# A short decoder trunk on one core: the weight buffers and the transposed branch outputs at another place modulo 1024 bytes

## The chip, the cores and the metric

The kernel runs on one core of a Trainium2 chip. The metric is device time in microseconds (us) of one execution. Three runs of the kernel before took 1026.52, 1027.38 and 1032.1 us, so the median is 1027.38.

## The reference, cut to what matters

Two layers act on 256 tokens of width 1024, all in float32. Each layer has a mixer and a feed-forward part:

```python
proj = einsum('bsd,dn->bsn', x, w_in)          # 11 parts: mLSTM q/k/v/o, DeltaNet qkv/z, two gates, ...
ha = mlstm(...);  hb = gated_delta(...)        # the two branches
y = sigmoid(gate_a) * (ha @ w_branch_a) + sigmoid(gate_b) * (hb @ w_branch_b)
x = layernorm(ALPHA * x + y @ w_out)
gt, up = split(x @ w_ffn_up)                   # 1024 -> 2 x 2816
x = layernorm(ALPHA * x + (silu(gt) * up) @ w_ffn_down)
```

Nearly all of the arithmetic is in the dense products with weights.

## The kernel before, in words

**Products.** A float32 product is made of three matmuls of the type float32r (`three`, L259): each operand is split into a rounded part (H) and the rest (L), and H.H, L.H and H.L are added up in PSUM. A matmul has a stationary operand, which a weight load of 128 columns brings into TensorE first, and a moving operand, which streams past it. The profile shows the two as PEld and PE.

**Weights.** They come from HBM in units of 128 x 1024 floats (`loading`, L213): a DMA into `raw`, a ScalarE copy that makes `wH`, a VectorE subtraction that makes `wL`. There is a ring of six pairs in the pool `hl` (L220). Further units go to spots that are free at the time: `wT0` to `wT3` in the pool `fix`, `wh0` to `wh2` in the pool of the feed-forward stage.

**Short and long matmuls.** In `chunkB` (L332) a 128-column slice of weights is stationary and the transposed activations (`xtH`, `xtL`, or the branch outputs `haH`/`haL` and `hbH`/`hbL`, transposed) move, 256 columns: the short matmuls. For each slice the order is H.H, L.H, H.L, so the weight loads are wH, wH, wL, and the streams xtH, xtL, xtH. In `chunkA` (L274) and `splitA` (L290) a 128-column slice of activations is stationary and 512 columns of weights move: the long matmuls. The second half of the last down projection is cut into pieces of 256 columns. The up projections (from 365 to 455 us and from 866 to 960 us) are chunkB in 9 of 11 chunks, 96 short matmuls each. The gate matmuls (`gates`, L415) are short ones whose stationary operand has 24 columns only.

**Order.** TensorE's order is written out by hand (`ORDER`, `PLAN`, L34 and L120). `arrange` (L1162) sets the order on VectorE, ScalarE and GpSimd from a cost per instruction (its element counts) and from which tiles share memory; where in memory a tile lies has no part in a cost.

**Places in SBUF.** Tiles of a pool lie one behind the other, each rounded up to 32 bytes a partition, in the order in which the program first asks for them; pools follow one another. `xtH` (8192 bytes a partition), `xtL` (8192), the constants (4096) and `x` (8192) are whole multiples of 1024, so all begin at the same place modulo 1024; call it 0. `mh` and `ph` (L172, L173) take 32 bytes each, so what follows begins at 64: the spots `T0` to `T3`, `raw`, the ring, all of whole multiples of 1024 bytes, and the pools M (mixer) and F (feed-forward), which begin at one address. In F come `lnp2`, `hH`, `hL` (multiples of 1024) and the spots `wh0` to `wh2`, all at 64. In M come `dm`, `TT`, `YY` (multiples of 1024), then `gnc` (4 bytes, so 32), `cw` (384), and the tags `vs` and `A`, at 64 + 32 + 384 = 480: `haH` and `hbH` lie there. Behind `A`, which is 32 bytes over a multiple of 1024, and `sv` (128 bytes), the other tags lie at 480 + 32 + 128 = 640, `C` among them: `haL` and `hbL`; the gate weights `wgH` and `wgL` too. The gate weights' slices are 96 bytes long, so they begin at 640, 736, 832, 928, then 0, 96, 192, 288. The transposed result of the branches' sum, `yH` and `yL`, has the spots `T0` and `T1`. A weight slice of 128 columns is 512 bytes, so it begins at its buffer's place or 512 after; a row of activations is 1024 bytes.

Of the kernel before, what the change touches and what calls it, by code (L numbers as in the profile page):

```python
# [12 lines left out]
F32 = mybir.dt.float32  # L13
# [4 lines left out]
P = 128  # L18
# [19 lines left out]
def chunk_order():  # L38
    return ORDER + ["wb", "wo"] + [f"up{j}" for j in range(UP)] + ["dn0", "dn1"]
# [93 lines left out]
class Net:  # L133
    def __init__(self, ctx, tc, a, dbg=None):
        self.tc, self.nc, self.a, self.dbg = tc, tc.nc, a, dbg
        nc = tc.nc
        self.fix = ctx.enter_context(tc.tile_pool(name="fix", bufs=1))
        self.raw = ctx.enter_context(tc.tile_pool(name="raw", bufs=4))
        self.hl = ctx.enter_context(tc.tile_pool(name="hl", bufs=6))
        self.pj = ctx.enter_context(tc.tile_pool(name="pj", bufs=4, space=bass.MemoryType.PSUM))  # L140
        self.sm = ctx.enter_context(tc.tile_pool(name="sm", bufs=4, space=bass.MemoryType.PSUM))
        self.dr = ctx.enter_context(tc.tile_pool(name="dr", bufs=2, space=bass.MemoryType.DRAM))
        self.u = 0
        self.clock = 0
        self.due = []
        self.lnt = {}
        self.ahead = []
        self.ring = 0
        self.busy = set()
        self.F = None  # L150
        self.t3 = False
        self.spots = {}
        n = 0
        for l in range(NL):
            for name in chunk_order():
                for i in range(COUNT.get(name, 4)):
                    spot = SPOTS.get((name, i))
                    if spot and (name != "va0" or l):
                        self.spots[n] = spot
                    n += 1  # L160
        fix = self.fix
        self.xt = [fix.tile([P, KT, S], F32R, name="xtH"), fix.tile([P, KT, S], F32R, name="xtL")]
        self.cst = fix.tile([P, 4 * P + 2 * S], F32, name="cst")
        c = self.cst
        self.idn = c[:, 0:P]
        self.tri = c[:, P:2 * P]
        self.one = c[:, 2 * P:3 * P]
        self.gm = c[:, 3 * P:4 * P]
        self.pm = c[:, 4 * P:4 * P + S]
        self.ei = c[:, 4 * P + S:4 * P + 2 * S]  # L170
        self.x = fix.tile([P, 2, D], F32, name="x")
        self.mh = fix.tile([P, 8], F32, name="mh")  # L172
        self.ph = fix.tile([P, 8], F32, name="ph")  # L173
        nc.gpsimd.memset(self.mh, -0.5)
        nc.gpsimd.memset(self.ph, 0.5)
        nc.vector.memset(self.x[:, 0, 0:P], 0.0)
        ps = self.sm.tile([P, 512], F32, name="sm")
        for i in range(WARM):
            self.mm(ps[:, 0:P], self.x[:, 0, 0:P], self.x[:, 0, 0:P], True, True)
# [235 lines left out]
    def gates(self, l, xt):  # L415
        nc, M = self.nc, self.M
        wg = M.tile([P, KT * 24], F32, name="wg", tag="jk", bufs=1)
        nc.sync.dma_start(out=wg, in_=self.a["wg"][l])
        sv = M.tile([P, 32], F32, name="sv")
        nc.sync.dma_start(out=sv, in_=self.a["sv"][l])  # L420
        wH = M.tile([P, KT * 24], F32R, name="wgH", tag="tmp")
        wL = M.tile([P, KT * 24], F32R, name="wgL", tag="dg")
# [475 lines left out]
    def mixer(self, l):  # L898
        nc, M, a = self.nc, self.M, self.a
        xt = self.xt  # L900
        mt = M.tile
# [9 lines left out]
            nc.gpsimd.memset(t, 0.0)  # L911
        st = [{}, {}]
        sm = {}
        self.gnc = mt([P, 1], F32, name="gnc")
        gates = self.gates(l, xt)
        cw = mt([P, 24, 4], F32, name="cw")
        self.gn = gn = mt([P, D], F32, name="gn", tag="vs", bufs=2)
# [12 lines left out]
        if l == 0:  # L930
            self.load_x()
            for n in range(2):
                pss = yield from self.chunkA(xt)
                for t in range(2):
                    put_v(n, t, pss[t])
                if n == 0:
                    self.load_c()
                    next(gates)
            consts()
        else:  # L940
            next(gates)
            consts()
            self.splitA(xt, [(4, 0), (4, 0)], put_v)
            self.t3 = False
# [413 lines left out]
```

## Time and profile before

| What | Value |
|---|---|
| Median of three runs | 1027.38 us (1026.52 to 1032.1) |
| The profiled execution: its own time | 1030.46 us |
| Its span, first to last instruction | 1028.5 us |
| TensorE matmuls, weight loads (busy) | 1011.6 us, 942.9 us |
| VectorE, ScalarE (busy) | 735.9 us, 596.8 us |
| Granted TensorE clock, mean | 0.999 |
| DMA | 183.61 MB, mean 179 GB/s |

Busy time of TensorE is the union of matmul records, whose ends are modelled: records of neighbouring matmuls overlap. How fast matmuls follow one another is read from their starts (the timeline) or from how many fall into a window, and the length of a record tells two paces apart.

### The profile page before, as it was taken

What the parts mean: (1) busy time and instruction counts of PE and PEld (TensorE: products, weight loads), DVE (VectorE), ACT (ScalarE), POOL (GpSimd) and SP (SyncE); (2) the same over time, 40 slices, a digit from 0 to 9 for tenths busy, and PEclk for the clock granted to TensorE, in tenths of its full rate; (3) what the DMA queues carried; (4) which work ended last, traced back from release to release, by engine and by line L of the source; (5) the groups of instructions that cost most, each with busy time, mean ns of one, the idle gap of its engine ahead of it and who ended that gap; (6) DMA issues with size and microseconds to landing.
All of it is one profiled execution on the core that took longest, in us unless ns stands there. A gap on an engine that the chain in (4) does not pass through costs nothing.

```text
span 1028.5 us, 18935 instructions
## 1 busy us (share of the span) xinstructions
PE 1011.6 (98%) x7474; PEld 942.9 (92%) x7474; DVE 735.9 (72%) x1313; ACT 596.8 (58%) x1110; POOL 46.9 (5%) x68
## 2 busy tenths in 40 slices
PE   8999999999999999999999999999999999999997
PEld 6999989989998899998889998998999989999886
DVE  4778998799668655556657699878985885555453
ACT  5658567866665445445545765767676554444440
POOL 1001000100000000000010100001000010000001
PEclk9999999999999999999999999999999999999999
DMA  8876235544556656667644742555355755666651
GB/s 272 286 218 197 71 134 185 185 143 138 175 184 241 204 166 189 199 187 229 217 128 154 261 148 82 188 170 159 101 191 159 257 189 179 190 187 187 185 164 41
DMA packets 57689, 183.61 MB, mean 179 GB/s; under 512 B 6657, under 2 KB 14337, under 8 KB 56961
## 3 DMA queue, kind: packets, MB, share of 16 engines
q1 hardware_dynamic: 50976, 179.13, 54.3%
q10 hardware_dynamic: 6624, 3.28, 1.2%
q8 instruction: 58, 0.95, 0.4%
q14 instruction: 31, 0.25, 0.1%
HBM read 181.21 MB, written 1.18 MB: 177 GB/s over the span
## 4 chain that ended last, share of the span: by engine, by line
PE 86%; DVE 7%; ACT 3%; DMA 2%; issue 1%; SPq 0%; POOL 0%; POOLq 0%; ACTq 0%; DVEq 0%
PE pj L257 78%; PE sm L257 6%; DMA raw<-in_ws 2%; DVE wL L233 1%; DVE stt L736 1%; DVE tmp L734 1%; PE sm L367 1%; ACT wH L232 1%; DVE cv L632 1%; PE sm L647 1%; DVE wt L551 0%; DVE ha L580 0%; POOL sq L576 0%; DVE vT L637 0%; PE sm L1092 0%
## 5 line engine op out<-in xcount | busy, mean ns | idle before, releaser
L233 DVE TENSOR_TENSOR wL<-raw,wH 128x1024 fp32r<-128x1024 f32 (+1 forms) x302 | 364.3, 1214 | 190.1 <-ACT wH L232 186.1
L232 ACT CAST wH<-raw 128x1024 fp32r<-128x1024 f32 (+1 forms) x302 | 314.7, 1044 | 228.0 <-PE pj L257 171.9
L257 PE MATMUL pj<-xtH,wH 128*128 128x256 f32 x1328 | 373.6, 281 | 0.0
L257 PE MATMUL pj<-xtH,wL 128*128 128x256 f32 x1328 | 368.9, 278 | 0.2 <-DVE wL L233 0.2
L257 PE MATMUL pj<-xtL,wH 128*128 128x256 f32 x1328 | 368.8, 278 | 0.0
L257 PEld LDWEIGHTS pj<-xtL,wH 128*128 128x128 f32 x1328 | 250.9, 189 | 0.3
L257 PEld LDWEIGHTS pj<-xtH,wH 128*128 128x128 f32 x1328 | 249.5, 188 | 0.9
L257 PEld LDWEIGHTS pj<-xtH,wL 128*128 128x128 f32 x1328 | 249.4, 188 | 0.4 <-DVE wL L233 0.4
L257 PE MATMUL pj<-wH,xtH 128*128 128x512 f32 x216 | 74.0, 403 | 3.0 <-ACT wH L232 2.9
L257 PE MATMUL pj<-wL,xtH 128*128 128x512 f32 x216 | 71.7, 392 | 0.1
L257 PE MATMUL pj<-wH,xtL 128*128 128x512 f32 x216 | 71.8, 392 | 0.0
L257 PE MATMUL pj<-wH,hH 128*128 128x512 f32 (+1 forms) x168 | 62.2, 370 | 0.0
L257 PE MATMUL pj<-wL,hH 128*128 128x512 f32 (+1 forms) x168 | 62.0, 369 | 0.0
L257 PE MATMUL pj<-wH,hL 128*128 128x512 f32 (+1 forms) x168 | 62.0, 369 | 0.0
L632 DVE SCALAR_TENSOR_TENSOR cv<-cu,cw,cv 128x255 f32<-128x255 f32 (+2 forms) x144 | 59.8, 475 | 2.9 <-ACT cv L630 2.8
L257 PEld LDWEIGHTS pj<-wH,xtH 128*128 128x128 f32 x216 | 39.4, 189 | 11.9 <-ACT wH L232 4.7
L257 PEld LDWEIGHTS pj<-wH,xtL 128*128 128x128 f32 x216 | 40.6, 188 | 9.1
L257 PEld LDWEIGHTS pj<-wL,xtH 128*128 128x128 f32 x216 | 40.5, 188 | 9.1 <-DVE wL L233 0.5
L734 DVE TENSOR_TENSOR tmp<-Mt,stt 128x248 f32<-128x248 f32 (+30 forms) x124 | 35.9, 289 | 2.9
L736 DVE TENSOR_TENSOR stt<-stt,tmp 128x248 f32<-128x248 f32 (+30 forms) x124 | 35.8, 289 | 2.7
L257 PEld LDWEIGHTS pj<-wH,hL 128*128 128x128 f32 x168 | 31.6, 188 | 5.3
L257 PEld LDWEIGHTS pj<-wH,hH 128*128 128x128 f32 x168 | 31.7, 189 | 5.3
(262 smaller groups left out, 1533.0 us busy)
## 6 DMA issues: line engine op xcount, KB each, us to landing
raw<-in_ws SPq DMA_DIRECT2D x322, 512.0 KB, 4.2
lnp<-in_ln SPq DMA_DIRECT2D x4, 1024.0 KB, 6.5
KQ<-rw ACTq DMA_DIRECT2D x8, 256.0 KB, 6.6
raw<-in_ws SPq DMA_DIRECT2D x4, 256.0 KB, 4.3
gn<-in_gn SPq DMA_DIRECT2D x2, 512.0 KB, 5.5
x<-in_x SPq DMA_DIRECT2D x1, 1024.0 KB, 10.0
mr<-rw ACTq DMA_DIRECT2D x4, 256.0 KB, 10.3
xraw<-in_xt SPq DMA_DIRECT2D x4, 128.0 KB, 3.8
```

Source lines behind the costliest of these rows:

```text
L232: nc.scalar.copy(out=h[:, sl], in_=r[:, sl])
L233: nc.vector.tensor_sub(out=lo[:, sl], in0=r[:, sl], in1=h[:, sl].bitcast(F32))
L257: self.nc.tensor.matmul(out, lhsT=l, rhs=r, start=start, stop=stop)
L367: self.nc.tensor.transpose(ps[:, i * P:(i + 1) * P], in_=src[:, i * P:(i + 1) * P], identity=self.idn)
L632: nc.vector.scalar_tensor_tensor(out=c[:, i, s:], in0=u[:, i, 0:S - s], scalar=cw[:, t, 3 - s:4 - s], in1=c[:, i, s:], op0=ALU.mult, op1=A ...
L647: self.nc.tensor.transpose(ps[:, h * P:h * P + P], in_=src[:, h, c * P:c * P + P], identity=self.idn)
L734: nc.vector.tensor_tensor(out=tmp[:, j + 1:, :], in0=mt[:, j + 1:, j:j + 1].to_broadcast([P, n, 8]), in1=stt[:, j:j + 1, :].to_broadcast([ ...
L736: nc.vector.tensor_tensor(out=stt[:, j + 1:, :], in0=stt[:, j + 1:, :], in1=tmp[:, j + 1:, :], op=ALU.subtract)
```

## The change

Three small tiles are made larger, and only their first part is used. `ph` takes 928 bytes in place of 32: all that follows it begins 896 bytes later, at 64 + 896 = 960 modulo 1024, that is 64 below 0. These are all weight buffers (ring, `raw`, spots), and with them `yH`, `yL`, `hH` and `hL`. `gnc` takes 704 bytes in place of 32, so tag `A` begins at 960 + 704 + 384 = 2048, place 0. `sv` takes 992 bytes in place of 128, so tag `C` begins at 0 + 32 + 992 = 1024, place 0 too. No instruction is added or taken away.

```diff
--- before.py
+++ after.py
@@ -170,7 +170,7 @@
         self.ei = c[:, 4 * P + S:4 * P + 2 * S]
         self.x = fix.tile([P, 2, D], F32, name="x")
         self.mh = fix.tile([P, 8], F32, name="mh")
-        self.ph = fix.tile([P, 8], F32, name="ph")
+        self.ph = fix.tile([P, 8 + 224], F32, name="ph")[:, 0:8]
         nc.gpsimd.memset(self.mh, -0.5)
         nc.gpsimd.memset(self.ph, 0.5)
         nc.vector.memset(self.x[:, 0, 0:P], 0.0)
@@ -416,7 +416,7 @@
         nc, M = self.nc, self.M
         wg = M.tile([P, KT * 24], F32, name="wg", tag="jk", bufs=1)
         nc.sync.dma_start(out=wg, in_=self.a["wg"][l])
-        sv = M.tile([P, 32], F32, name="sv")
+        sv = M.tile([P, 248], F32, name="sv")[:, 0:32]
         nc.sync.dma_start(out=sv, in_=self.a["sv"][l])
         wH = M.tile([P, KT * 24], F32R, name="wgH", tag="tmp")
         wL = M.tile([P, KT * 24], F32R, name="wgL", tag="dg")
@@ -911,7 +911,7 @@
             nc.gpsimd.memset(t, 0.0)
         st = [{}, {}]
         sm = {}
-        self.gnc = mt([P, 1], F32, name="gnc")
+        self.gnc = mt([P, 176], F32, name="gnc")[:, 0:1]
         gates = self.gates(l, xt)
         cw = mt([P, 24, 4], F32, name="cw")
         self.gn = gn = mt([P, D], F32, name="gn", tag="vs", bufs=2)
```

## Rows read from the trace of the kernel before

**Rows 1.** The page's parts 1 and 2: busy time by engine, and the granted clock.

```profile
span 1028.5 us, 18935 instructions
PE 1011.6 (98%) x7474; PEld 942.9 (92%) x7474; DVE 735.9 (72%) x1313; ACT 596.8 (58%) x1110; POOL 46.9 (5%) x68
...
PEclk9999999999999999999999999999999999999999
```

**Rows 2.** The page's part 4, the chain that ended last: shares by engine, by line.

```profile
PE 86%; DVE 7%; ACT 3%; DMA 2%; issue 1%; SPq 0%; POOL 0%; POOLq 0%; ACTq 0%; DVEq 0%
PE pj L257 78%; PE sm L257 6%; DMA raw<-in_ws 2%; DVE wL L233 1%; DVE stt L736 1%; DVE tmp L734 1%; PE sm L367 1%; ACT wH L232 1%; DVE cv L632 1%; PE sm L647 1%; DVE wt L551 0%; DVE ha L580 0%; POOL sq L576 0%; DVE vT L637 0%; PE sm L1092 0%
```

**Rows 3.** The waits of TensorE, longest in total first: us, times, longest.

```profile
PE pj L257 <- ACT wH L232: 2.9, 3, 1.4
...
```

**Rows 4.** Two windows of TensorE matmuls: us, busy (count), granted clock, DMA.

```profile
370.00:450.00 80.00, 80.00 (x709) 1.00 0.63 194
875.00:955.00 80.00, 80.00 (x682) 1.00 0.61 185
```

**Rows 5.** Groups by line in 370 to 450 us (layer 0): count, busy us, mean ns, idle.

```profile
L257 PE MATMUL pj<-xtL,wH 128*128 128x256 f32 x236 | 65.1, 276 | 0.0
L257 PEld LDWEIGHTS pj<-xtL,wH 128*128 128x128 f32 x236 | 44.3, 188 | 0.0
```

**Rows 6.** The same groups in 875 to 955 us (layer 1).

```profile
L257 PE MATMUL pj<-xtL,wH 128*128 128x256 f32 x227 | 63.8, 281 | 0.0
L257 PEld LDWEIGHTS pj<-xtL,wH 128*128 128x128 f32 x227 | 43.6, 192 | 0.0
```

**Rows 7.** Timeline near 378 us: start us, length us, engine, line, operation.

```profile
377.91 0.28 PE L257 MATMUL pj<-xtH,wL 128*128 128x256 f32 x1
377.92 0.19 PEld L257 LDWEIGHTS pj<-xtH,wH 128*128 128x128 f32 x1
378.03 0.28 PE L257 MATMUL pj<-xtH,wH 128*128 128x256 f32 x1
```

**Rows 8.** Groups of TensorE over the whole run, each shape apart; columns as before.

```profile
L257 PE MATMUL pj<-xtH,wL 128*128 128x256 f32 x1328 | 368.9, 278 | 0.2 <-DVE wL L233 0.2
L257 PE MATMUL pj<-xtL,wH 128*128 128x256 f32 x1328 | 368.8, 278 | 0.0
...
L257 PE MATMUL pj<-wH,xtL 128*128 128x512 f32 x216 | 71.8, 392 | 0.0
L257 PE MATMUL pj<-wL,xtH 128*128 128x512 f32 x216 | 71.7, 392 | 0.1
...
L257 PE MATMUL pj<-wH,hL 128*128 128x512 f32 x136 | 53.0, 389 | 0.0
...
L257 PE MATMUL pj<-hbL,wH 128*128 128x256 f32 x128 | 35.9, 281 | 0.0
L257 PE MATMUL pj<-haL,wH 128*128 128x256 f32 x128 | 35.9, 281 | 0.0
...
L257 PE MATMUL pj<-wH,hL 128*128 128x256 f32 x32 | 9.1, 283 | 0.0
```

**Rows 9.** Timeline of TensorE, branch product, layer 0: first and eleventh matmul.

```profile
295.78 0.28 PE L257 MATMUL pj<-hbL,wH 128*128 128x256 f32 x1
...
296.96 0.28 PE L257 MATMUL pj<-hbH,wL 128*128 128x256 f32 x1
```

**Rows 10.** Timeline of TensorE: the gate matmuls of layer 0.

```profile
31.35 0.28 PE L257 MATMUL sm<-xtH,wgH 128*24 128x256 f32 x1
...
31.59 0.28 PE L257 MATMUL sm<-xtH,wgL 128*24 128x256 f32 x1
...
32.62 0.28 PE L257 MATMUL sm<-xtH,wgL 128*24 128x256 f32 x1
...
32.97 0.28 PE L257 MATMUL sm<-xtH,wgL 128*24 128x256 f32 x1
...
33.31 0.28 PE L257 MATMUL sm<-xtH,wgL 128*24 128x256 f32 x1
```

## The prediction

> **What bounds the kernel now.** [...] A busy share does not say that matmuls run at their best pace, so next the chain that ended last: 78% of it is one line of matmuls into the projection banks, the split-float products of weights with activations, and 6% the small matmuls of the mixer [rows 2]. Then TensorE's waits: the longest item is 2.9 us in three waits [rows 3]. So nothing outside TensorE sets the time. What a matmul takes is the time, and the change touches nothing but where its two operands lie.
>
> Now the same work in two places. The up projections of layers 0 and 1 are the same instructions on buffers at the same places. In 80 us the trace counts 709 matmuls in layer 0 and 682 in layer 1, both at clock 1.00 [rows 4]. A record lasts 276 to 281 ns and they start every 113 to 118 ns, so some 2.4 of each count are cut by the edges: 80/706.6 is 113.2 ns, 80/679.6 is 117.7 ns. The records say the same: 276 ns each and 188 for a weight load in layer 0 [rows 5], 281 and, for one load in three, 192 in layer 1 [rows 6]. There are two rhythms, then, 4.5 ns apart, and 5 ns of record are 4.5 ns of spacing (0.9). A weight load starts with the matmul before it: load at 377.92 us, that matmul at 377.91 [rows 7]. So the load of 128 columns (512 bytes) reads while the matmul streams 256 columns (1024 bytes). Both read at once, at different paces, from places fixed by the layout.
>
> By the sizes in the code, weights lie 64 bytes above the transposed activations modulo 1024 (the load reads at +64, or +576 for odd column blocks). The branch outputs lie 480 (hi) and 640 (lo) above the activations, so that there the load reads 416 and 576 below the stream, or 512 more.
>
> **Which rows price placement.** The branch products never run at 113: ten spacings span 295.78 to 296.96 us, 118.0 ns each [rows 9], and over the run their records average 35.9/128 = 280.5 ns [rows 8]. The long matmuls, where the weights stream and the activations are loaded, last 392 ns with the activations 64 below the weights, but 389 ns with the up-projection result at the same place as the weights [rows 8]. The 256-column pieces of the down projection, load 512 above the stream, last 283 ns [rows 8]. So placement has a price of 0 to 7 ns of record per matmul.
>
> **The change, part by part.** (1) The three padded tiles add no instruction, no transfer and no wait; the order of work on every queue stays, since sizes of small tiles enter no cost in the order. Zero; what hides behind TensorE stays hidden, the largest wait being 2.9 us [rows 3].
>
> (2) The 3 x 1328 = 3984 short matmuls on the activations go from +64/+576 to -64/+448. Two of the three forms average 368.9/1328 and 368.8/1328, 277.75 ns (the third opens each unit, so its mean holds waits too) [rows 8]. 1.75 of 5 ns above 276 puts 35% of them into the slow rhythm, 1.6 ns each. Bounds for the new place: 276 as in rows 5 (-3984 x 1.6 = -6.3 us); 281 as in rows 6 (+3984 x 2.9 = +11.6); 283 as in the pieces (7 x 0.9 = 6.3 ns, so +3984 x 4.7 = +18.7). I take 276. The stream covers 1024 bytes while the load covers 512. At +64 it starts below the load and must pass it in the first part of each matmul, where a slip in the start moves the meeting; at -64 it starts ahead and draws away. And 276 is no accident of one place: the long form without a cost, 389 ns, is that of two short spacings. This is the weakest step.
>
> (3) The 2 x 3 x 128 = 768 branch matmuls get the same distances as (2). At 113.2 instead of 118.0 that is 768 x 4.8 = -3.7 us; at 117.7, nothing; at the pieces' price +768 x 1.5 = +1.2.
>
> (4) The long matmuls on activations, 3 x 216 = 648 from the ring, go from -64 to +64. Today's excess is 392 - 389 = 3 ns of record, 2.7 of spacing. Bounds: all of it gone, -1.7 us; twice of it, +1.7. I take zero: no row shows a long matmul at +64.
>
> (5) Those of the down and output projections move with the weights: distance as before, zero. The small matmuls of the mixer shift too, unpriced; they are 6% of the chain [rows 2], so 1% of them is 0.6 us either way. I take zero.
>
> **Sum.** The profiled execution took 1030.46 us: -6.3 - 3.7 = -10.0, so 1020.5. That execution is 3.1 above the median, 1027.38. An estimate from rows 4: one up projection's 9 x 96 = 864 short matmuls in the slow rhythm cost 864 x 4.5 = 3.9 us, as much as it lies above the fastest run (1026.52). So much of the first term is already absent from the median run, and 1020.5 is 6.9 us, 0.7%, below that.
>
> **Rivals.**
> A is the forecast: fast rhythm everywhere, 1017 to 1023.
>
> B: *the start still decides*. If both rhythms remain possible at -64, the mix stays, and only the branch matmuls gain by joining it, 768 x 3.2 = 2.5 us: 1027.4 - 2.5 = 1025 (1022 to 1030). For it: rows 5 and 6, one layout with both. Against: the branch matmuls have one pace only, so a layout can settle it.
>
> C, the other side: *the load trails and still collides*. Place: every short matmul; price: the slow rhythm for all, 1030.46 + 11.6, so 1042, 1050 at the pieces' price. It decides once most of the short ones are at 281 ns. For it, and this is the strongest row against me: the gate matmuls, whose load is 24 columns, start 119 ns apart with the load 384 below the stream (31.35 to 31.59, two), 114 to 115 with it 288 to 96 below (31.59 to 32.62, nine), and 113 with it 96 above (32.97 to 33.31, three) [rows 10]. Loads below the stream cost something there. The long matmuls at -64 also cost [rows 8], though only their first part meets a load. Against: these loads are short or meet a longer stream, and -64 itself is in no short row except a third of the branch products.
>
> D: *placement plays no part*, or the allocator does not put the tiles where the sizes say: 1027.4. [...] Rows 8 and 9 speak against it: same shapes, same clock, other places, 118.0 against 113.2.
>
> **Chances.** A measurement of this kernel can tell about 0.5% from no change: the lines are 1022.2 and 1032.5. A 0.42, B 0.21, C 0.31, D 0.06. A lies under the lower line but for 0.04; B gives 0.04 to faster; C gives 0.01 to the middle. Faster 0.38 + 0.04 = 0.42; same 0.04 + 0.17 + 0.06 + 0.01 = 0.28; slower 0.30. Range 1016 to 1043: it leaves out the far half of C (0.15) and a little below A (0.03). A's own range is 1017 to 1023.
>
> **What would show it.** Right: both up projections near 709 matmuls in 80 us, records of 276 ns and loads of 188 in all forms, branch records 276, TensorE's waits as now. A wrong: one up projection at 276 and the other at 281 (B); 281 or more in both (C); branch records still at 280.5 with the rest unchanged (D). Long matmuls at 389 or at 395 show which bound of (4) holds. New TensorE waits above 3 us would say that (1) was wrong.

## The result, and the profile after

The changed kernel takes **1039.69 us** (median of four, 1039.32 to 1039.97). The kernel before, in four executions beside it, took 1028.93 (1026.52 to 1032.1). The ratio is 1.0112, interval 1.0092 to 1.0132: slower by 1.1%. The profiled execution took 1039.88 us, 9.4 above the profiled one of before.

The page of the kernel after: parts 1 and 2 in part, and part 4, the chain that ended last.

```profile
span 1038.0 us, 18935 instructions
...
PE 1023.6 (99%) x7474; PEld 952.6 (92%) x7474; DVE 736.3 (71%) x1313; ACT 597.0 (58%) x1110; POOL 46.9 (5%) x68
...
PEclk9999999999999999999999999999999999999999
...
PE 92%; DVE 5%; DMA 1%; ACT 1%; issue 0%; SPq 0%; POOL 0%; POOLq 0%; DVEq 0%; ACTq 0%
```

Same number of instructions, VectorE and ScalarE as they were; TensorE has 12 us more of busy time and a larger share of the chain [rows 1, 2]. The granted clock differs in one place. Window 15 to 20 us, kernel before, then after (us, busy and count, granted clock, DMA):

```profile
15.00:20.00 5.00, 4.94 (x22) 1.00 0.78 255
15.00:20.00 5.00, 4.95 (x15) 0.66 0.79 268
```

In the profile after, six long matmuls there start 426 to 427 ns apart instead of 233, at a granted clock of 0.50 from 15.6 to 18.2 us, which is 1.2 us of the difference between the two profiles. That it comes from the change is not shown: the mean clock is 0.997 in the profile after and 0.999 in that of before, but 0.997 too in another profile of the kernel before (`before_again`, below). The waits of TensorE in the kernel after, the two longest in total:

```profile
PE pj L257 <- ACT wH L232: 2.9, 3, 2.3
PE sm L257 <- ACT dm L751: 1.4, 3, 0.9
```

No new wait: the longest item is again 2.9 us [rows 3]. So the matmuls themselves became slower. The two windows of the up projections, kernel after:

```profile
370.00:450.00 80.00, 80.00 (x682) 1.00 0.60 185
875.00:955.00 80.00, 80.00 (x681) 1.00 0.60 184
```

Layer 0 fell from 709 to 682, layer 1 stayed at the slow pace [rows 4]. Some 2.4 matmuls of a count are cut by the edges, so 682 means 80/679.6, 117.7 ns from one start to the next, and 709 means 113.2. The groups in 370 to 450 us of the kernel after:

```profile
L257 PE MATMUL pj<-xtL,wH 128*128 128x256 f32 x228 | 63.6, 279 | 0.0
L257 PE MATMUL pj<-xtH,wL 128*128 128x256 f32 x227 | 63.6, 280 | 0.0
```

279 to 280 ns where rows 5 had 276. TensorE's groups over the whole run, kernel after, each shape apart:

```profile
L257 PE MATMUL pj<-xtH,wL 128*128 128x256 f32 x1328 | 370.8, 279 | 0.0
L257 PE MATMUL pj<-xtL,wH 128*128 128x256 f32 x1328 | 370.2, 279 | 0.0
...
L257 PE MATMUL pj<-wL,xtH 128*128 128x512 f32 x216 | 73.2, 399 | 0.1
L257 PE MATMUL pj<-wH,xtL 128*128 128x512 f32 x216 | 72.8, 397 | 0.0
...
L257 PE MATMUL pj<-wH,hL 128*128 128x512 f32 x136 | 52.9, 389 | 0.0
...
L257 PE MATMUL pj<-hbL,wH 128*128 128x256 f32 x128 | 35.8, 279 | 0.0
...
L257 PE MATMUL pj<-wH,hL 128*128 128x256 f32 x32 | 9.1, 283 | 0.0
```

Against rows 8: the short ones on the activations 278 to 279 ns, the long ones 392 to 397 and 399, the branch ones 281 to 279, and nothing where the distance stayed (389, 283). The branch product of layer 0, kernel after, timeline of TensorE:

```profile
297.63 0.28 PE L257 MATMUL pj<-hbL,wH 128*128 128x256 f32 x1
...
298.81 0.28 PE L257 MATMUL pj<-hbH,wL 128*128 128x256 f32 x1
```

Ten spacings in 1.18 us: 118, as in rows 9, not the 113 that was forecast.

**Where the time went.** A record's end is modelled, so the account is made of starts: the intervals from each matmul's start to the next, summed by kind over the profiled execution. What an interval has beyond 126 ns (short) or 240 ns (long) is counted as a gap.

| Kind (intervals) | before, us | after, us | difference |
|---|---|---|---|
| short, on activations (4032) | 463.8 | 473.0 | +9.2 |
| long, on activations (768) | 176.5 | 179.4 | +2.9 |
| branch (768 products, 64 transposes of their outputs) | 97.3 | 96.9 | -0.4 |
| long and pieces of down and output projections (785) | 164.4 | 164.4 | 0.0 |
| small ones of mixer and gates (1056) | 92.1 | 92.1 | 0.0 |
| gaps, waits among them | 25.6 | 23.4 | -2.2 |

The sum is 9.5 us, as the span; nearly all of the 1.2 us of the lower clock stands among the gaps of after. Mean spacing without gaps: short 114.8 to 117.2 ns, long 229.3 to 233.3.

### The profile page after: what moved, and what is told of

It reads as the page before. It is cut to its first block, busy times and chain, and to the rows that moved or that the text cites. A ratio compares the mean times of both kernels' runs of the same rounds, so it can differ in the third digit from the quotient of the medians.

```text
span 1038.0 us, 18935 instructions
## 1 busy us (share of the span) xinstructions
PE 1023.6 (99%) x7474; PEld 952.6 (92%) x7474; DVE 736.3 (71%) x1313; ACT 597.0 (58%) x1110; POOL 46.9 (5%) x68
## 3 DMA queue, kind: packets, MB, share of 16 engines
HBM read 181.21 MB, written 1.18 MB: 176 GB/s over the span
## 4 chain that ended last, share of the span: by engine, by line
PE 92%; DVE 5%; DMA 1%; ACT 1%; issue 0%; SPq 0%; POOL 0%; POOLq 0%; DVEq 0%; ACTq 0%
PE pj L257 83%; PE sm L257 7%; PE sm L367 1%; DVE tmp L734 1%; PE sm L647 1%; DVE stt L736 1%; DVE wL L233 1%; DMA raw<-in_ws 1%; DVE cv L632 1%; ACT wH L232 0%; DVE ha L580 0%; DVE wt L551 0%; POOL sq L576 0%; DVE vT L637 0%; SPq L186 0%
## 5 line engine op out<-in xcount | busy, mean ns | idle before, releaser
L736 DVE TENSOR_TENSOR stt<-stt,tmp 128x248 f32<-128x248 f32 (+30 forms) x124 | 35.9, 290 | 2.7
L257 PEld LDWEIGHTS pj<-wL,hH 128*128 128x128 f32 x168 | 31.7, 189 | 5.3
```

Of the source, the lines that this page charges most:

```text
L257: self.nc.tensor.matmul(out, lhsT=l, rhs=r, start=start, stop=stop)
L736: nc.vector.tensor_tensor(out=stt[:, j + 1:, :], in0=stt[:, j + 1:, :], in1=tmp[:, j + 1:, :], op=ALU.subtract)
```

## The experiments

Tables give mean spacings worked out in the same way. A **stretch** below is a row of short matmuls (branch products among them) between two breaks (other matmuls or a wait); it is called fast if its last nine spacings average below 114.3 ns and slow above 117. In the profiles of before and after each of the 57 stretches on the activations alone keeps its pace from its sixth spacing to its end: any three spacings in a row average within 0.8 ns of the last nine, which average 113.3 or 117.8. The two longest are those of the up projections, 839 matmuls each in one pace: 839 x 4.45 ns = 3.7 us between fast and slow.

Three rows of the kernel before change their distance on the way, and each changes its pace there. One that passes from the activations to a branch output; three starts, ten matmuls apart:

```profile
184.41 0.28 PE L257 MATMUL pj<-xtH,wL 128*128 128x256 f32 x1
185.54 0.28 PE L257 MATMUL pj<-haH,wH 128*128 128x256 f32 x1
186.72 0.28 PE L257 MATMUL pj<-haL,wH 128*128 128x256 f32 x1
```

113 ns on the activations, 118 on the branch output, with no wait between. The two others pass the other way, from 118 to 113.

**The kernel before once more** (no edit).

> The kernel before, unchanged, for a second trace. Start theory (at +64 both rhythms are open, and how a stretch begins decides which one it keeps): the stretches that run at 113.3 ns and at 117.8 ns are not the same ones as in the first trace; above all the layer 1 up projection may be at 276 ns records this time, and each up projection that changes sides moves the time by 864 x 4.5 = 3.9 us, within 1026 to 1033 us. Place theory (the distance alone fixes the rhythm): the same stretches as before, so 281 ns in layer 1 and 276 ns in layer 0 again, and 1030 us.

1030.30 us, with 708 and 681 matmuls in the two windows, short spacing 114.9: the profile of before repeats, layer 0 fast and layer 1 slow. The start theory's guess, other long stretches, did not come; but two paces at one distance are no place theory either, so a beginning that the program nearly fixes was left, and the later runs test it.

**Only the branch outputs moved**, weights at +64 as before:

```diff
-        sv = M.tile([P, 32], F32, name="sv")
+        sv = M.tile([P, 248], F32, name="sv")[:, 0:32]
-        self.gnc = mt([P, 1], F32, name="gnc")
+        self.gnc = mt([P, 144], F32, name="gnc")[:, 0:1]
```

> Only the branch half of the change: the weights stay 64 above the activations, the branch outputs move to the place of the activations, so their loads read at +64 too. Place theory: the branch records fall from 280.5 to the mix of the short matmuls at +64, 276 to 281 ns, worth 0 to 3.7 us; the long ones stay at 392 ns; total 1024 to 1030 us. Start theory: the same for the branch matmuls, and the short ones fall into either rhythm anew. If instead the branch half were what costs, the total would be 1035 us or more.

> The branch half alone again, now timed. Place theory: the branch matmuls near 114.3 instead of 118.3 ns save 744 x 4 = 3.0 us in every run, so a ratio near 0.997, with a spread of some 4 to 8 us as before, since both rhythms stay open at +64 and an up projection that changes sides moves 3.9 us. If the one run at 1023.9 was a lucky start only, the ratio is 1.000 within its interval.

One execution took 1023.92 us; in nine more the median is 1026.32 (1023.98 to 1030.83) against 1030.0, ratio 0.9963 (0.9949 to 0.9978). The two windows of the profiled one among the nine, 1030.83 us:

```profile
370.00:450.00 80.00, 80.00 (x682) 1.00 0.61 185
875.00:955.00 80.00, 80.00 (x708) 1.00 0.63 196
```

And of its groups over the whole run a branch one:

```profile
L257 PE MATMUL pj<-haL,wH 128*128 128x256 f32 x128 | 35.5, 277 | 0.0
```

Branch products at +64 run at 277 ns where rows 8 had 281, so this half of the change gains by itself; 0.4% in the median. And layer 0's up projection is slow here, though nothing of it was touched: the single execution had both fast (709 and 702; its second window reaches past the projection's end). These are the sides that it takes from one execution to the next.

**Distances.** Weights at eight other places, branch outputs at the activations' place throughout. The edit is that of the change with other sizes, for +0:

```diff
-        self.ph = fix.tile([P, 8], F32, name="ph")
+        self.ph = fix.tile([P, 248], F32, name="ph")[:, 0:8]
-        sv = M.tile([P, 32], F32, name="sv")
+        sv = M.tile([P, 248], F32, name="sv")[:, 0:32]
-        self.gnc = mt([P, 1], F32, name="gnc")
+        self.gnc = mt([P, 160], F32, name="gnc")[:, 0:1]
```

The others have, for `ph` and `gnc` in floats, 256 and 152 (+32), 16 and 136 (+96), 24 and 128 (+128), 40 and 112 (+192), 48 and 104 (+224), 56 and 96 (+256), 72 and 80 (+320).

> Weights at the place of the activations modulo 1024, branch outputs there too, so loads read at 0 or 512 from the stream. Place theory: the long matmuls fall to 389 ns (as the down projection at this distance), 2.7 ns x 648 = 1.7 us; the short ones take a price of their own, between 276 and the 283 ns of the 256-column pieces at 512; if 283, 3984 x 4.7 = 18.7 us more, 1047 us, if 276, 1019 us. Start theory: a mix of 276 and 281 ns again, 1020 to 1040 us.

> Weights 256 above the activations, branch outputs at their place. The load starts a quarter of a stream row ahead, so the stream passes it in the middle of its way. Place theory: one price for all short matmuls; the nearest gate matmuls (load 288 above) ran at 113.3, so 276 ns records and about 1020 us, if the narrow loads tell it rightly. Start theory: both rhythms again, 1020 to 1040 us. Long matmuls: between 389 and 399 ns.

> Weights 192 above the activations, that is -64 plus 256. Period 256: as the changed kernel: short matmuls mostly at 117.8 ns, long ones at 397 to 399 ns, 1039 to 1040 us. Period 128: as +64: a mix nearer to 113.3 ns, long ones at 392 to 394 ns, 1023 to 1032 us. Period 512: a price of its own.

> Weights 320 above the activations, that is +64 plus 256. Period 256: as the branch-only kernel (distance +64 for all): both rhythms, long ones at 392 to 396 ns, 1022 to 1030 us. Period 512: a price of its own. Start theory: whatever it is, the same places in the program need not keep the same rhythm.

> Weights 32 above the activations. Of the distances modulo 256 tried, 0 gives 120.0 ns alone, 64 both rhythms, 96 and 128 some 118.7 ns, 192 (the changed kernel) both rhythms but mostly 117.8. If only the two distances at a quarter and three quarters of the period open the 113.3 ns rhythm, +32 has one slow rhythm, 118 to 120 ns, and takes 1040 to 1046 us. If the range around +64 opens it, a mix again, 1020 to 1032 us.

> Weights 96 above the activations, 32 bytes off the steps of 64 tried so far; the gate matmuls with a load 96 above ran at 113.3 ns each. If the narrow loads tell it rightly: 276 ns records everywhere, 1018 to 1021 us. If half a step of 64 bytes makes every load straddle, one slower rhythm of 118 to 120 ns, as the branch outputs had before at a place 32 off the steps of 64 (480), and 1038 to 1046 us.

> Weights 128 above the activations, branch outputs at their place. The prices repeat every 128, 256 or 512 bytes of distance; +0 and +256 gave one and the same rhythm, 120.0 ns (283 ns records). Period 128: 120.0 ns again, long matmuls 389 to 392 ns, 1045 us. Period 256: a price of its own, since +128 is then half a period from +0; 113 to 120 ns, 1018 to 1045 us.

> Weights 224 above the activations, that is -32 modulo 256. If only distances of 64 and 192 open the fast rhythm: one slow rhythm, 118 to 120 ns, 1040 to 1046 us. If distances below 256 down to 192 share the changed kernel's way: mostly 117.8 ns and 1040 us. A time under 1022 us would name a place better than both kernels.

One execution each, in order of the distance modulo 256. The kernel before took 1033.92 us beside 0 and 256, 1030.0 (median) beside 32 and 224, 1029.47 beside 96, 128, 192 and 320, so the spacings tell more than single times:

| Weights above the activations | us | windows | short, ns | long, ns | fast stretches |
|---|---|---|---|---|---|
| 0 | 1044.58 | 669, 669 | 119.9 | 227.7 | 0 of 71 |
| 256 | 1046.99 | 669, 669 | 119.9 | 227.7 | 0 of 71 |
| 32 | 1043.65 | 679, 678 | 118.3 | 233.2 | 0 of 71 |
| 64 (before) | 1030.46 | 709, 682 | 114.8 | 229.3 | 49 of 72 |
| 320 | 1028.0 | 681, 709 | 115.2 | 229.4 | 47 of 72 |
| 96 | 1043.08 | 676, 677 | 118.5 | 233.3 | 0 of 71 |
| 128 | 1042.56 | 677, 677 | 118.8 | 232.6 | 0 of 71 |
| 192 | 1040.12 | 682, 682 | 117.4 | 233.3 | 4 of 71 |
| 960, that is -64 (after) | 1039.88 | 682, 681 | 117.2 | 233.3 | 6 of 72 |
| 224 | 1035.59 | 689, 688 | 116.8 | 233.2 | 0 of 72 |

At 224 most stretches lie between the two limits, at 116.7. The times of about 1020 us that 96 and 256 were to take if the narrow loads of the gate matmuls [rows 10] priced wide ones were missed by more than 20 us in both.

Two whole-run groups of four of these kernels, a short and a long one. Weights at +0:

```profile
L257 PE MATMUL pj<-xtL,wH 128*128 128x256 f32 x1328 | 375.6, 283 | 0.0
...
L257 PE MATMUL pj<-wH,xtL 128*128 128x512 f32 x216 | 71.4, 391 | 0.0
```

Weights at +256:

```profile
L257 PE MATMUL pj<-xtL,wH 128*128 128x256 f32 x1328 | 375.6, 283 | 0.0
...
L257 PE MATMUL pj<-wH,xtL 128*128 128x512 f32 x216 | 72.0, 394 | 0.0
```

Weights at +192:

```profile
L257 PE MATMUL pj<-xtL,wH 128*128 128x256 f32 x1328 | 370.5, 279 | 0.0
...
L257 PE MATMUL pj<-wH,xtL 128*128 128x512 f32 x216 | 72.6, 396 | 0.0
```

Weights at +320:

```profile
L257 PE MATMUL pj<-xtL,wH 128*128 128x256 f32 x1328 | 369.4, 278 | 0.0
...
L257 PE MATMUL pj<-wH,xtL 128*128 128x512 f32 x216 | 71.7, 392 | 0.0
```

Three pairs 256 bytes apart agree in both kinds: 0 with 256 (records of 283 ns short; 227.7 ns spacing of the long, though their records, with modelled ends, read 391 and 394), 192 with 960 (279, 233.3), 64 with 320 (278, 229.3 and 229.4). So in these three pairs **the distance modulo 256 goes with the pace**: "64 below" ran as "192 above", windows of 682 and 681 against 682 and 682. Of the places tried, +64 (and +320, the same modulo 256) is the only one where most stretches are fast. At 192 fast stretches exist but are few. At 0 the short matmuls are at their slowest and the long ones at their fastest: the two kinds rank the places differently.

**Only the weights moved** (the first edit of the change alone):

```diff
-        self.ph = fix.tile([P, 8], F32, name="ph")
+        self.ph = fix.tile([P, 232], F32, name="ph")[:, 0:8]
```

> Only the first part of the change: all weight buffers 64 below, the branch outputs kept at their old distance from the weights. Period-256 theory: short matmuls on the activations as in the changed kernel, mostly 117.8 ns, long ones 233.3 ns, branch matmuls at 118.3 as before; 0.4 us more than the changed kernel, 1040 us. If the branch half were to blame for some of the loss, the total would be below 1037 us.

> The first edit of the change alone again (weights at -64, branch outputs at their old distance), now timed. One profile of it took 1031.25 us, with both up projections at 709 matmuls in 80 us, where the whole change took 1039.7 with both at 682, at the same distance of the same operands in those stretches. If the rhythm of a stretch is set by how it begins, and that is fixed by the program: a narrow spread near 1031, ratio to before about 1.001. If it is set anew in each execution: times that fall into steps of 3.7 us between 1031 and 1039, and the profile shows at least one up projection at 682. If the first look was an accident: 1039, ratio 1.009 to 1.012.

One execution took 1031.25 us. Its windows:

```profile
370.00:450.00 80.00, 80.00 (x708) 1.00 0.63 192
875.00:955.00 80.00, 80.00 (x708) 1.00 0.64 195
```

Nine more took 1037.62 (1031.58 to 1042.19), ratio 1.0081 (1.0054 to 1.0109). The profiled one of these, 1040.32 us, had:

```profile
370.00:450.00 80.00, 80.00 (x682) 1.00 0.60 185
875.00:955.00 80.00, 80.00 (x682) 1.00 0.61 183
```

One program, the same places, 9 us apart between its two profiles, 7.4 of which (2 x 3.7) are the two long stretches. The two were taken on two chips; but the nine executions, all on one, spread as far. So at -64 the distance does not force the slow pace: 708 and 708 stand in one profile, 682 and 682 in the other. The single execution was neither typical nor an accident of measurement: of the nine two lie within 1 us of it, the rest between 1035 and 1042.

This run also tells the distance from the weights' own place. The branch outputs moved along with the weights here, and their products kept their pace: 118.3 ns as in the kernel before, in both profiles. A group of the second:

```profile
L257 PE MATMUL pj<-haL,wH 128*128 128x256 f32 x128 | 35.9, 281 | 0.0
```

It is the line of rows 8, 35.9 and 281; with the weights at the same -64 but the branch outputs at the activations' place (the whole change) the pace was 117.8.

**Other beginnings, same places.** The transposes of the first up-projection results, which TensorE does between matmuls just ahead of the long stretches, come a step later or earlier (`later(n, ...)` puts them off by n steps of the order of work; among the long matmuls a step is six of them):

```diff
-            self.later(2, flip)
+            self.later(3, flip)
```

> The whole change, with the transposes of the first up-projection results one step later, so that the long stretches of short matmuls begin after other matmuls. Distances are those of the change. If the distance of -64 sets the rhythm: both up projections stay at 682 in 80 us, 1039 to 1040. If the beginning of a stretch sets it: either both stay at 682 (this beginning is no better), or one or both go to 709 and the time falls by 3.7 us for each, to 1036 or 1032.

> The whole change, with the same transposes one step earlier. As the run before: the distance alone gives 682 and 682 and 1039 to 1040 again; the beginning of a stretch can give 709 in one or both, 3.7 us less for each. A run of either kind with 709 at a distance of -64 speaks against the distance as what sets the rhythm of the stretch.

The whole change with a step later: **1032.01 us** (1030.56 to 1033.3, ten executions), ratio 1.003 (1.0014 to 1.0045). Its windows:

```profile
370.00:450.00 80.00, 80.00 (x708) 1.00 0.63 192
875.00:955.00 80.00, 80.00 (x708) 1.00 0.62 192
```

Both long stretches became fast at the distance of the change, and the median fell by 7.7 us, where two times 3.7 were expected. The step earlier (`later(1, flip)`) took 1045.23 (1042.34 to 1048.86), ratio 1.016 (1.0128 to 1.0191). Its windows:

```profile
370.00:450.00 80.00, 80.00 (x708) 1.00 0.61 191
875.00:955.00 80.00, 80.00 (x682) 1.00 0.57 173
```

Its longest wait of TensorE:

```profile
PE sm L1092 <- DVE fhA L1087: 6.2, 6, 1.3
```

One long stretch fast here, too, but the transposes now come before VectorE has their input: 6.2 us of waits, new ones, are more than that gain. As a price of the beginning this run says little; that 708 stands at -64 again, it does say.

**The same step at +64**, once with the branch outputs moved, once in the kernel before:

> The branch outputs alone moved (weights at +64 as before), with the transposes one step later. Without that step the branch outputs alone gave 1026.3 us and 0.9963, with the up projections at 709 and 709 in one profile, 682 and 709 in another. If the beginning of a stretch sets its rhythm: a shift of whole up projections, 3.7 us each, so 1024 where both begin fast and 1031 where both begin slow, with less spread. If the beginning plays no part: 1026.3 with the same spread.

> The kernel before with the transposes of the first up-projection results one step later; distances as before. With that step the whole change went from 682 and 682 matmuls in 80 us to 709 and 709, and by 7.7 us. If the beginning of the long stretches is what spreads the kernel before over 1025 to 1033 (709 and 682 in its profile): both at 709, a narrower spread, 3 to 4 us below the slower of its own runs and about 2 us below its median of 1028. If it plays no part at +64: 1028, the same spread, one stretch at 682.

With the branch outputs moved: 1025.02 us against 1027.97, ratio 0.9966 (0.9949 to 0.9983); apart from one execution of 2051, 1023.67 to 1027.41. The kernel before with this step alone: **1026.02 us** (1024.19 to 1027.28, twelve executions) against 1029.35 (1026.05 to 1032.76), ratio 0.9966 (0.9954 to 0.9979). Windows of the latter:

```profile
370.00:450.00 80.00, 80.00 (x708) 1.00 0.63 193
875.00:955.00 80.00, 80.00 (x708) 1.00 0.62 194
```

Both fast, and the spread of before shrinks from 6.7 to 3.1 us: most of it, as far as the profiles tell, was the up projections changing sides. Three versions now beat both kernels (branch outputs alone 0.9963, the step alone 0.9966, both 0.9966), and the runs can't rank them. That the two do not add up has a reason in the spacings: with both, the branch products gain (118.3 to 114.6 and 116.9 ns), but the short ones on the activations stand at 114.3 against 113.9 with the step alone, 4032 x 0.4 = 1.6 us back, since other stretches began slow. These spacings are from one profile of each.

**The whole change once more** (no edit).

> The whole change, unedited, in more executions. It had 1039.3 to 1040.0 in four, all that the two slow stretches give, while the weights alone at the same distance went from 1031.6 to 1042.2 in nine. If the whole program fixes the beginning of the long stretches: 1039 to 1040 again in nearly all, 682 and 682 in the profile. If each execution sets it anew: times in steps of 3.7 us down to 1032, and a median below 1039.

1039.87 us (1039.01 to 1041.62, six executions), ratio 1.0101 (1.0081 to 1.0121), windows 682 and 682. In ten executions of the change none came below 1039. For this program the slow beginning is all but fixed, as the fast one is with the transposes a step later; for the weights alone it is not.

## Why the prediction was wrong

Forecast 1020.5 us and faster; measured 1039.69, slower and near rival C (1042). It lies inside the range only because the range took in the near half of C; the forecast's own rival A had 1017 to 1023.

**The failed step is (2)**: "At +64 it starts below the load and must pass it in the first part of each matmul, where a slip in the start moves the meeting; at -64 it starts ahead and draws away", and from that 276 ns and -6.3 us. Measured: +9.2 us. The picture needed places to matter over 1024 bytes; in the runs places 256 apart agreed, -64 with 192 (117.2 and 117.4 ns), and there 6 of 72 and 4 of 71 stretches were fast, where 49 of 72 were at +64. Over the profiles at each place: 46 to 49 at +64 and +320, 3 to 9 at -64 and +192. The bounds, +11.6 for the slow rhythm in all, were right, and the choice between them was made by a picture that no row supported, against rows 10. Those pointed the right way here but were no price either: at 96, where their narrow loads ran at 113 ns, the loads of 128 columns took 118.5. One row of the prediction did hold a point of the table of distances, unread: the pieces with the load 512 above the stream, 0 modulo 256, had 283 ns, and so have the short ones at +0 and +256.

**What the loss is made of.** One more long stretch slow (layer 0): 3.7 us. The other short stretches: 9.2 - 3.7 = 5.5. The long matmuls: 2.9. The branch: -0.4. The gaps, 2.2 less in sum, gave that back. The kernels with the long stretches fast at both places, after and before with the later transposes, confirm the part that is not the up projections: their profiled executions are 1032.30 - 1026.39 = 5.9 us apart, of which 4032 x (115.2 - 113.9) = 5.2 in the short and 768 x (233.3 - 229.2) = 3.1 in the long; the branch gave 0.4 back, the gaps and the small matmuls 2.0.

**Point by point.** (1) Right: no new wait, no other order. (3) Wrong: -3.7 was forecast, -0.4 came, since the branch products took the slow pace of the new distance (117.8 ns); its bound for that pace, nothing, was about right. At +64 the gain is there: 114.1 to 116.9. (4) Mis-sized: zero, within 1.7 either way, was taken from "twice" an excess of 2.7 ns; measured is an excess of 6.6 (233.3 - 226.7, two fast short spacings) and +2.9 us. A load 64 above the stream costs more here than one 64 below it (233.3 ns against 229.3). (5) Right: 164.4 us and 92.1 us before and after.

The reading of the profiled execution of before, 3.1 us above the median because one up projection was slow, held: with both fast the profiled execution took 1026.39, 4.1 less.

**Rivals.** B, *the start still decides*, was right that both rhythms remain possible at -64 (682 and 681 in the change, 708 and 708 with the transposes a step later). Its price failed because it kept the mix of before: 49 of 72 stretches were fast at +64, 6 of 72 at -64. C was right about the time, and wrong that the load below the stream forces the slow pace: at 0, 32, 96, 128 and 224 no stretch was fast, at -64 some were. D fell: the same short matmuls on the activations started every 113.3 to 119.9 ns with their two operands at other places.

**What stays open.** Why the places of the two operands change the pace was not shown: no run read one operand without the other, and no record shows where a read stands within a matmul. Nor was it found what in the beginning picks the pace: with the transposes a step later, the 24 short matmuls, two transposes and 839 short ones stand in the same order as before, and what moved lies further ahead. The last spacing ahead of the transposes was 116 to 118 ns in the profiles with slow stretches of the weights at -64 and 118 to 120 in those with fast ones, which overlaps and settles nothing.

## What to carry to other kernels

Where TensorE is the bound, look at the place of a weight buffer against the streamed operand, which here was worth up to 6% of a short float32r matmul (113.3 to 119.9 ns); compare distances modulo 256 bytes, since three pairs 256 apart agreed here, and measure each one, since a picture of who leads and who trails ranked them wrongly. Split such a change by buffer: one half of this one gained 0.4%, the other cost 0.8%. And count matmuls in equal windows of several profiles before pricing a pace: if one program shows two, a small reordering ahead of the long stretches may be worth about as much as the layout: here 7.7 us of the 10.8 lost at -64, and 0.3% at +64, where the layout of the branch outputs gave 0.4%.

## What the runs showed of the hardware that was not expected

- The spacing of a 256-column float32r matmul with a 128-column weight load, at a granted clock of 1.00, went with the distance of the two operands modulo 256 bytes at the places tried: 119.9 at 0 and 256; 118.3 to 118.8 at 32, 96 and 128; 116.8 at 224; two paces, 113.3 and about 117.8, at 64, 192, 320 and 960.
- With two paces at one distance, a stretch held one of them from its sixth spacing on, 839 matmuls long in the up projections, at a granted clock of 1.00, and one program took either (the weights alone: 708 and 708 in one profile, 682 and 682 in the other). Where the distance changed inside a row, the pace changed with it (113 to 118 ns at 185.54 us of the kernel before).
- The 512-column form ranked the places otherwise: 227.7 ns at 0 and 256, 229.3 with the weights at +64 and +320, 232.6 to 233.3 at the others.
